# A hybrid attention and HGRN2 layer on one core: the query projection moved behind the last HGRN head, twelve opening matmuls on a constant tile, first loads reordered

## The chip, the cores and the metric

The kernel runs on one core of one Trainium2 chip. The metric is the device time of one execution in microseconds, as the median of several runs. The engines are named as the profile names them: PE is TensorE (matrix products, PEld its weight loads), DVE is VectorE, ACT is ScalarE, POOL is GpSimd, SP is SyncE, whose queue issues all the DMAs here.

## The reference, cut to what matters

One decoder layer over 1024 tokens of width 1024. The input projection makes the queries `q` (512 columns), three pairs of keys and values of 128 columns each for the compressed (`kc_raw`, `vc_raw`), selected and window branches, 24 gate logits, and four blocks of 512 columns for the HGRN2 heads.

```python
h = rms_norm(x, norm_mix[l])
proj = h @ w_in[l]
(q, kc_raw, vc_raw, ks, vs, kw, vw, gate_logits, hq, hf, hi, hg) = jnp.split(proj, split_points, axis=-1)
q = rms_norm(q.reshape(B, T, H, dh), q_norm[l])
kc = rms_norm(compress(kc_raw..., cmp_pos_k[l], cmp_k_w1[l], cmp_k_w2[l]), k_norm[l, 0])
vc = compress(vc_raw..., cmp_pos_v[l], cmp_v_w1[l], cmp_v_w2[l])
...
o_nsa = nsa_mixer(q, kc, vc, ks, vs..., kw, vw..., gates)
o_hgrn = hgrn2_mixer(hq, hf, hi, hg, lower_bounds[l], hgrn_o_norm[l])
x = x + jnp.concatenate([o_nsa, o_hgrn], axis=-1) @ w_out[l]
h = rms_norm(x, norm_ffn[l])
gate, up = jnp.split(h @ w_gate_up[l], 2, axis=-1)
x = x + (jax.nn.silu(gate) * up) @ w_down[l]
```

The queries are needed first by the attention blocks, the norms of the queries too; HGRN2 does not use them.

## The kernel before, in words

Every product in float32 accuracy is made of three products of split operands: `split` (lines 107 to 114) makes a rounded high part on ACT and the rest on DVE, and `mm3` (lines 116 to 119) issues high x high, high x low and low x high into one PSUM bank. So the lines 117, 118 and 119 are those of nearly all matmuls, 110 and 111 those of weight splits (113 and 114 of the transposed input).

The program runs in this order.

1. **Opening and wide stages** (pool `p0`). `step(c)` loads chunk c of the transposed input (`x_in`) into a page of `kv1` and splits it into `hT_h` and `hT_l`. `wide(n0, ...)` takes 512 columns of `w_in` for all eight token tiles at once, one PSUM bank each, chunk by chunk: 8 chunks x 8 tiles x 3 = 192 matmuls. It is called for the gate columns of HGRN (`C_HG`, line 319), the queries (`C_Q`, line 320) and the values of HGRN (`C_HI`, line 321). `ev_q` (line 311) evacuates a query tile into `qtok` on ACT, squares it on POOL (line 314) and sums it by heads on DVE (line 315); the last tile is followed by `rsqrt` into `rs_q`.
2. **HGRN heads 0 to 3** (pool `hg`, lines 438 to 465). `dim_tile` makes a head's columns, `hgrn_head` runs seven levels (`lv`): each has four 128x128 products on PE (line 381), whose operands ACT has gathered (line 377), and on DVE and POOL two scalings (lines 386, 387), one product of `fp` (line 389) and two masked copies into the head's matrix `At` (line 392). Eight transposes (line 399), state products (line 406), output products (lines 418, 420), a norm, and eight closing transposes (line 435) with their evacuation (line 436) follow. `At` is page 4 or 5 of `kv1`, by the head's parity; page 7 is `rs_b`, the broadcast row scale, last read by the head's first steps.
3. **Compressed branch** (pool `cp`, from line 511 on, opened after `hg` is closed). `tok_group` makes 256 columns for the compressed branch (`C_KC`: keys and values; eight token tiles of 24 matmuls, one after the other through the two banks `a0` and `a1` that `acc()` gives in turn), `ev_c` (line 516) evacuates them into two tiles `kcv` of pool `cp`. `comp_gather(which)` transposes them, copies them into `kk` (lines 535, 543, 545) and multiplies by `w1t` (line 557); `comp_gelu` and `comp_out` follow. Between these stand the groups for window and selected keys and values (`kv_group`), their norms (`keys_norm`) and transposes (`keys_out`).
4. **Attention blocks**, out projection, norm and feed-forward part.

A scheduler sets each engine's order: it may move an instruction ahead of others where its operands allow it, and keeps the written order otherwise as a priority. A tile waits until the memory it takes over is free: `cp` takes over what `hg` leaves. Weight pages come from a ring of eight (`wring`), raw loads from three pages (`raw`).

## Time and profile before

| | us |
|---|---|
| median of three runs | 1428.98 |
| lowest and highest run | 1428.91, 1430.2 |
| the profiled execution's own time | 1426.9 |
| its span, first to last instruction | 1424.9 |
| TensorE busy | 1374.1 |
| VectorE busy | 1048.4 |
| ScalarE busy | 597.3 |
| GpSimd busy | 390.6 |

The span is that of one profiled execution; its own time has 2.0 us more around it. Busy times add up durations on one engine, so what bounds the kernel at a place is read from that place: from the stretches, the waits and the timeline there.

### The profile page before, as it was taken

The numbers are of one execution on the slowest core, as the hardware profiler recorded it, in microseconds if no ns is written. First come the engines' busy times: TensorE is split into PE (matmuls) and PEld (weight loads), VectorE is DVE, ScalarE is ACT, GpSimd is POOL, SyncE is SP. The second block draws the span as 40 slices with busy tenths as digits, with TensorE's granted clock in tenths as the row PEclk, the third lists the DMA queues.
The fourth block names the chain that finished last, engine by engine and source line by source line (L and its number), as shares of the span: only waits on it lengthen the run. The fifth ranks groups of instructions, "written<-read, shape, count | busy, mean of one in ns | idle before, by whom it ended". The sixth has DMA issues, their size and how long they took to land.

```text
span 1424.9 us, 19708 instructions
## 1 busy us (share of the span) xinstructions
PE 1374.1 (96%) x7080; PEld 1135.3 (80%) x7080; DVE 1048.4 (74%) x1895; ACT 597.3 (42%) x1156; POOL 390.6 (27%) x341
## 2 busy tenths in 40 slices
PE   8999999969999999999998999999999999999998
PEld 6888788859987778777776788888888888887787
DVE  5331588872777887888876898888888887589864
ACT  7222233313436666666664433333333333443342
POOL 0020011110025442434354533233323320058500
PEclk9999999979999999999999999999999999999999
DMA  9311110102130001100003233333333337997431
GB/s 339 106 45 46 44 28 21 30 1 75 47 134 1 1 1 32 43 31 16 30 16 89 67 112 111 111 111 101 99 112 97 111 111 245 328 323 277 150 109 59
DMA packets 108625, 135.72 MB, mean 95 GB/s; under 512 B 6096, under 2 KB 63600, under 8 KB 108528
## 3 DMA queue, kind: packets, MB, share of 16 engines
q1 hardware_dynamic: 108528, 134.46, 28.3%
q8 instruction: 56, 0.92, 0.3%
q14 instruction: 41, 0.34, 0.1%
HBM read 105.87 MB, written 28.57 MB: 94 GB/s over the span
## 4 chain that ended last, share of the span: by engine, by line
PE 83%; DVE 11%; ACT 3%; issue 2%; POOL 1%; DMA 1%; SPq 0%; ACTq 0%; POOLq 0%; DVEq 0%
PE bank L117 9%; PE bank L118 9%; PE bank L119 9%; PE a L117 8%; PE a L118 8%; PE a L119 8%; PE ps_t L118 4%; PE ps_t L119 4%; PE ps_t L117 4%; PE ps_t L846 3%; PE a L850 2%; DVE wop L111 2%; PE a L851 2%; PE ps_t L381 2%; PE ps_s L824 1%
## 5 line engine op out<-in xcount | busy, mean ns | idle before, releaser
L110 ACT ACTIVATE wop<-rpage 128x512 fp32r<-128x512 f32 x140 | 87.6, 629 | 190.9 <-PE a L119 78.6
L835 POOL TENSOR_SCALAR pbig<-pbig,den,gates 128x640 f32<-128x640 f32 (+7 forms) x128 | 104.0, 817 | 165.7 <-DVE den L834 146.5
L111 DVE TENSOR_TENSOR wop<-rpage,wop 128x512 fp32r<-128x512 f32 x140 | 106.9, 766 | 49.7 <-ACT wop L110 47.7
L849 DVE TENSOR_TENSOR ph<-ps_t,ph 128x512 fp32r<-128x512 f32 x126 | 84.3, 683 | 17.8 <-ACT ph L848 17.0
L848 ACT ACTIVATE ph<-ps_t 128x512 fp32r<-128x512 f32 x126 | 72.7, 596 | 48.9 <-PE ps_t L846 39.2
L846 PE MATMUL ps_t<-ident,pbig 128*128 128x128 f32 x504 | 78.2, 274 | 2.1 <-POOL pbig L835 2.1
L111 DVE TENSOR_TENSOR wop<-act_a,wop 128x512 fp32r<-128x512 f32 x48 | 47.4, 988 | 32.5 <-ACT wop L110 32.5
L387 POOL TENSOR_TENSOR kp<-kp,fp 128x256 f32<-128x256 f32 x28 | 20.0, 716 | 183.9 <-PE bank L364 129.7
L997 POOL TENSOR_TENSOR tmp<-tmp,rpage 128x512 f32<-128x512 f32 x21 | 31.2, 1488 | 142.4 <-DVE wop L111 142.4
L846 PEld LDWEIGHTS ps_t<-ident,pbig 128*128 128x128 f32 x504 | 60.6, 140 | 11.6 <-POOL pbig L835 3.2
L111 DVE TENSOR_TENSOR wlo<-wraw,whi 128x1024 fp32r<-128x1024 f32 (+2 forms) x23 | 27.1, 1182 | 54.2 <-ACT whi L110 22.5
L833 ACT ACTIVATE pbig<-ps_s,nm 128x640 f32<-128x640 f32 (+3 forms) x64 | 55.9, 875 | 23.5 <-DVE nm L832 17.8
L118 PE MATMUL bank<-wop 128*128 128x512 f32 x165 | 64.9, 394 | 0.0
L117 PE MATMUL bank<-wop 128*128 128x512 f32 x165 | 64.9, 393 | 0.0
L119 PE MATMUL bank<-wop 128*128 128x512 f32 x165 | 64.7, 392 | 0.0
L110 ACT ACTIVATE wop<-act_a 128x512 fp32r<-128x512 f32 x48 | 30.3, 631 | 81.4 <-PE bank L119 56.6
L832 DVE TENSOR_REDUCE nm<-ps_s 128x1 f32<-128x640 f32 (+3 forms) x64 | 58.1, 913 | 4.4 <-PE ps_s L827 3.0
L850 PE MATMUL a<-ph,kv 128*128 128x512 f32 x132 | 58.6, 444 | 2.0 <-ACT ph L848 1.2
L851 PE MATMUL a<-ph,kv 128*128 128x512 f32 x132 | 56.9, 431 | 3.2 <-DVE ph L849 2.7
L111 DVE TENSOR_TENSOR wop<-tmp,wop 128x512 fp32r<-128x512 f32 x42 | 43.6, 1039 | 20.6 <-ACT wop L110 20.0
L957 POOL TENSOR_TENSOR tmp<-rpage 128x512 f32<-128x512 f32 x20 | 26.0, 1301 | 112.9 <-DMA rpage<-in_w_gate_up_dram 112.9
L110 ACT ACTIVATE wop<-tmp 128x512 fp32r<-128x512 f32 x42 | 26.6, 634 | 70.4 <-POOL tmp L997 37.5
(457 smaller groups left out, 4458.1 us busy)
## 6 DMA issues: line engine op xcount, KB each, us to landing
rpage<-in_w_gate_up_dram SPq DMA_DIRECT2D x86, 256.0 KB, 3.1
raws<-in_w_down_dram SPq DMA_DIRECT2D x35, 512.0 KB, 7.2
act_a<-act_d SPq DMA_DIRECT2D x12, 1024.0 KB, 6.2
act_d<-as SPq DMA_DIRECT2D x33, 256.0 KB, 2.1
act_e<-act_d SPq DMA_DIRECT2D x6, 1024.0 KB, 8.0
act_d<-tmp SPq DMA_DIRECT2D x22, 256.0 KB, 2.1
act_d<-th SPq DMA_DIRECT2D x22, 256.0 KB, 2.1
xn<-in_x_dram SPq DMA_DIRECT2D x8, 512.0 KB, 5.3
```

What stands on the lines that cost most here:

```text
L110: A.activation(hi, src, AF.Copy)
L111: V.tensor_tensor(lo, src, hi.bitcast(F32), op=OP.subtract)
L117: PE.matmul(o, ah, bh, start=first, stop=False, skip_group_check=chained)
L118: PE.matmul(o, ah, bl, start=False, stop=False, skip_group_check=chained)
L119: PE.matmul(o, al, bh, start=False, stop=last, skip_group_check=chained)
L832: V.tensor_reduce(nm, sv, axis=AX.XY, op=OP.max, negate=True)
L835: G.tensor_scalar(pp, pp, den, gates[:, qb, h * 3 + 1 + b:h * 3 + 2 + b], op0=OP.mult, op1=OP.mult)
L846: PE.transpose(pt[:, r * P:(r + 1) * P], wts[r][:, c0:c0 + P], ident)
L848: A.activation(ph[:, 0], pt, AF.Copy)
L849: V.tensor_tensor(ph[:, 1], pt, ph[:, 0].bitcast(F32), op=OP.subtract)
L850: PE.matmul(o, vst[b][:, kb, g, :], ph[:, 0], start=b == 0 and kb == kb0, stop=False)
L851: PE.matmul(o, vst[b][:, kb, g, :], ph[:, 1], start=False, stop=False)
```

## The change

It does four things. The wide query stage and the squares in it are taken out of the opening; the queries are made by `tok_group` instead, tiles 0 to 3 behind the compressed columns, tiles 4 and 5 after the first gelu, 6 and 7 after the second, and their squares follow in `query_norms`. The compressed columns' group moves into the HGRN pool's block, and `kcv` becomes pages 4 and 7 of `kv1`. The window key groups come after the queries, and `comp_keys` is called earlier. At the opening a constant tile is filled and twelve matmuls are made on it into PSUM banks whose content nothing reads; the first weight tile is loaded ahead of the first chunk of x, and that chunk is loaded in pieces of 256, 256 and 512 columns. One line more at the top moves all line numbers, which are in the new file one higher up to the opening.

```diff
@@ -38,6 +38,7 @@
 EXTRA = 1
 LATE = 4
 KEEP = 0
+WARM = 12
 NFIRST = 2
 EARLY = (-4, -3, -2, -1)
 C_Q, C_KC, C_VC, C_KS, C_VS, C_KW, C_VW, C_G, C_HQ, C_HF, C_HI, C_HG = (
@@ -250,6 +251,11 @@
         ssx = p0.tile([P, NT], F32, name="ssx")
         nc.sync.dma_start(par_t, par)
 
+        warm = p0.tile([P, 512], BF16, name="warm")
+        V.memset(warm, 1.0)
+        for _ in range(WARM):
+            PE.matmul(ps_t(), warm[:, 0:P], warm, start=True, stop=True)
+
         def x_stats(t):
             xn = p0.tile([P, D], F32, name="xn", tag="xn", bufs=2)
             nc.sync.dma_start(xn, x[0, t * P:(t + 1) * P, :])
@@ -258,11 +264,10 @@
                 rsqrt(rsx, ssx, NT, 1.0 / D, EPS)
                 V.tensor_scalar(rsh, rsx, 0.5, None, op0=OP.mult)
 
-        def x_in(c, pieces):
-
-            w = T // pieces
-            for k in range(pieces):
-                sl = slice(w * k, w * (k + 1))
+        def x_in(c, cuts):
+
+            for k0, k1 in zip(cuts, cuts[1:]):
+                sl = slice(k0, k1)
                 nc.sync.dma_start(kv1[:, 4 + c % 4, sl], x_t[c * P:(c + 1) * P, sl])
                 split(hT_h[:, c, sl], hT_l[:, c, sl], kv1[:, 4 + c % 4, sl], gmx[:, c:c + 1])
 
@@ -280,9 +285,9 @@
             banks = [bank8() for _ in range(NT)]
             ws = w_steps(n0, fine)
             for c in range(NK):
+                wh, wl = next(ws)
                 if step:
                     step(c)
-                wh, wl = next(ws)
                 for t in range(NT):
                     mm3(banks[t], hT_h[:, c, t * P:(t + 1) * P], hT_l[:, c, t * P:(t + 1) * P], wh, wl,
                         c == 0, c == NK - 1)
@@ -290,7 +295,7 @@
                         evac(t, banks[t])
 
         def step(c):
-            x_in(c, 2 if c == 0 else 1)
+            x_in(c, (0, 256, 512, T) if c == 0 else (0, T))
             if c >= 2:
                 x_stats(c - 2)
 
@@ -306,18 +311,7 @@
             V.scalar_tensor_tensor(gmix[:, :, t * P:(t + 1) * P], th.rearrange("p (h n) -> p h n", h=4), 1.0,
                                    a.rearrange("p (h n) -> p h n", h=4), op0=OP.add, op1=OP.mult)
 
-        ssq = p0.tile([P, 64], F32, name="ssq")
-
-        def ev_q(t, a):
-            A.activation(qtok[:, t, :], a, AF.Copy, scale=rsx[:, t:t + 1])
-            jq = p0.tile([P, 512], F32, name="jq", tag="th", bufs=2)
-            G.tensor_tensor(jq, qtok[:, t, :], qtok[:, t, :], op=OP.mult)
-            V.tensor_reduce(ssq[:, t * 8:(t + 1) * 8], jq.rearrange("p (h d) -> p h d", d=DH), axis=AX.X, op=OP.add)
-            if t == NT - 1:
-                rsqrt(rs_q, ssq, 64, 1.0 / DH, EPS)
-
         wide(C_HG, ev_g, step, True)
-        wide(C_Q, ev_q)
         wide(C_HI, ev_v)
 
         for k in range(2):
@@ -435,6 +429,14 @@
                 PE.transpose(st[:, c * P:(c + 1) * P], qp[:, (4 * k + c) * P:(4 * k + c + 1) * P], ident)
             A.activation(gmix[:, h, sl], st, AF.Copy, scale=og)
 
+    def queries(order, group, parts=None):
+
+        def ev(t, a):
+            A.activation(qtok[:, t, :], a, AF.Copy, scale=rsx[:, t:t + 1])
+        parts = parts or in_units([(C_Q, 512)], 512, (0, 2, 4, 6, 8))
+        group(parts, 512, ev, order, acc)
+        return parts
+
     with tc.tile_pool(name="hg", bufs=2) as hp:
         def head(h):
             fp = hp.tile([P, T], F32, name="fp")
@@ -464,6 +466,13 @@
         head(2)
         head(3)
 
+        def ev_c(t, a):
+            A.activation(kcv[t // 4].rearrange("p (t n) -> p t n", n=256)[:, t % 4], a[:, 0:256], AF.Copy,
+                         scale=rsx[:, t:t + 1])
+        kcv = kv1[:, 4, :], kv1[:, 7, :]
+        tok_group(in_units([(C_KC, 256)], 256), 256, ev_c)
+        parts_q = queries(range(4), tok_group)
+
 
     dram = ctx.enter_context(tc.tile_pool(name="dram", bufs=1, space=bass.MemoryType.DRAM))
     x1_d = dram.tile([T, D], F32, name="x1_d")
@@ -510,11 +519,6 @@
 
     with tc.tile_pool(name="cp", bufs=1) as cp:
         kcn = cp.tile([P, GROUPS, P], F32R, name="kcn")
-        kcv = [cp.tile([P, 4, 256], F32, name=f"kcv{k}") for k in range(2)]
-
-        def ev_c(t, a):
-            A.activation(kcv[t // 4][:, t % 4], a[:, 0:256], AF.Copy, scale=rsx[:, t:t + 1])
-        tok_group(in_units([(C_KC, 256)], 256), 256, ev_c)
         V.memset(kcn.bitcast(F32), 0.0)
         V.memset(kc_st.bitcast(F32), 0.0)
         V.memset(vc_st.bitcast(F32), 0.0)
@@ -546,7 +550,7 @@
             for hf in range(2):
                 pt = ps_t()
                 for t in range(4):
-                    src = kcv[hf][:, t, which * P:(which + 1) * P]
+                    src = kcv[hf][:, 256 * t + which * P:256 * t + (which + 1) * P]
                     if t % 2:
                         PE.matmul(pt[:, t * P:(t + 1) * P], src, swap, start=True, stop=True)
                     else:
@@ -601,9 +605,13 @@
             V.tensor_copy(kc_st[:, 0:128].rearrange("p (g n) -> p g n", g=GROUPS),
                           pk[:, 0:256].rearrange("p (g n) -> p g n", g=GROUPS)[:, :, 0:64])
 
-        kv2 = big.tile([P, NK, T], F32R, name="kv2", tag="KV")
-        kst = {(b, g): kv2[:, 2 * b + g, :] for b in range(2) for g in range(GROUPS)}
-        vst = [kv2[:, 4 + 2 * b:6 + 2 * b, :].rearrange("p a (t g e) -> p (a t) g e", t=4, g=GROUPS) for b in range(2)]
+        def query_norms():
+            ssq = small.tile([P, 64], F32, name="ssq", tag="ssq", bufs=1)
+            for t in range(NT):
+                jq = cp.tile([P, 512], F32, name="jq", tag="jq", bufs=2)
+                G.tensor_tensor(jq, qtok[:, t, :], qtok[:, t, :], op=OP.mult)
+                V.tensor_reduce(ssq[:, t * 8:(t + 1) * 8], jq.rearrange("p (h d) -> p h d", d=DH), axis=AX.X, op=OP.add)
+            rsqrt(rs_q, ssq, 64, 1.0 / DH, EPS)
 
         def kv_weights(b):
             ncols = (256, 280)[b]
@@ -651,19 +659,26 @@
 
         ph0, w20 = comp_gather(0)
         w0 = comp_gelu(ph0)
-        parts1 = kv_weights(1)
-        kraw10 = kv_group(1, 0, parts1)
+        queries((4, 5), tok_group, parts_q)
         ph1, w21 = comp_gather(1)
         comp_out(0, w0, w20)
         w1 = comp_gelu(ph1)
+        queries((6, 7), tok_group4, parts_q)
+        comp_out(1, w1, w21)
+        kv2 = big.tile([P, NK, T], F32R, name="kv2", tag="KV")
+        kst = {(b, g): kv2[:, 2 * b + g, :] for b in range(2) for g in range(GROUPS)}
+        vst = [kv2[:, 4 + 2 * b:6 + 2 * b, :].rearrange("p a (t g e) -> p (a t) g e", t=4, g=GROUPS) for b in range(2)]
+
+        query_norms()
+        parts1 = kv_weights(1)
+        kraw10 = kv_group(1, 0, parts1)
+        comp_keys()
+        kd10 = keys_norm(1, 0, kraw10)
         kraw11 = kv_group(1, 1, parts1)
-        comp_out(1, w1, w21)
-        kd10 = keys_norm(1, 0, kraw10)
+        keys_out(1, 0, kd10)
         parts0 = kv_weights(0)
         kd11 = keys_norm(1, 1, kraw11)
         kraw00 = kv_group(0, 0, parts0)
-        keys_out(1, 0, kd10)
-        comp_keys()
         keys_out(1, 1, kd11)
         kd00 = keys_norm(0, 0, kraw00)
         kraw01 = kv_group(0, 1, parts0)
```

Three places of the engines' orders, first as they were and then as they are.

TensorE in HGRN head 3, from the first level on (line 381, in the new file 375, is a level's products; `a_2356` and `a_2095` are banks of the compressed columns, lines 117 to 119 and 118 to 120 their three products). Before:

```order
L381 MATMUL ps_t<-qp,kv_86 128x128 x4
L117 MATMUL a_2356<-whi,hT_h 128x256
L118 MATMUL a_2356<-wlo,hT_h 128x256
L119 MATMUL a_2356<-whi,hT_l 128x256
L117 MATMUL a_2356<-whi,hT_h 128x256
L118 MATMUL a_2356<-wlo,hT_h 128x256
L119 MATMUL a_2356<-whi,hT_l 128x256
L381 MATMUL ps_t<-qp,kv_86 128x128 x24
L399 MATMUL bank<-ident,kp 128x128 x8
L406 MATMUL bank<-kv_86,kp 128x128 x7
L418 MATMUL bank<-kv_86 128x128 x2
```

After:

```order
L375 MATMUL ps_t<-qp,kv_86 128x128 x4
L120 MATMUL a_2095<-whi,hT_l 128x256
L118 MATMUL a_2095<-whi,hT_h 128x256
L119 MATMUL a_2095<-wlo,hT_h 128x256
L120 MATMUL a_2095<-whi,hT_l 128x256
L118 MATMUL a_2095<-whi,hT_h 128x256
L119 MATMUL a_2095<-wlo,hT_h 128x256
L120 MATMUL a_2095<-whi,hT_l 128x256
L118 MATMUL a_2095<-whi,hT_h 128x256
L375 MATMUL ps_t<-qp,kv_86 128x128 x4
L119 MATMUL a_2095<-wlo,hT_h 128x256
L120 MATMUL a_2095<-whi,hT_l 128x256
```

The other six levels stood back to back; now matmuls of the compressed columns stand between each two of them, and in the same way ahead of the closing transposes.

TensorE around head 3's closing transposes (line 435, now 429; `a_2382` is the third tile of the compressed columns, `a_2225` the seventh). Before:

```order
L420 MATMUL bank<-fp,qp 128x128
L435 MATMUL bank<-ident,qp 128x128 x8
L117 MATMUL bank<-whi,hT_h 128x280
L118 MATMUL bank<-wlo,hT_h 128x280
L119 MATMUL bank<-whi,hT_l 128x280
L117 MATMUL bank<-whi,hT_h 128x280
L118 MATMUL bank<-wlo,hT_h 128x280
L117 MATMUL a_2382<-whi,hT_h 128x256
L118 MATMUL a_2382<-wlo,hT_h 128x256
```

After:

```order
L120 MATMUL a_2225<-whi,hT_l 128x256
L118 MATMUL a_2225<-whi,hT_h 128x256
L119 MATMUL a_2225<-wlo,hT_h 128x256
L429 MATMUL bank<-ident,qp 128x128 x4
L120 MATMUL a_2225<-whi,hT_l 128x256
L429 MATMUL bank<-ident,qp 128x128 x4
L118 MATMUL a_2225<-whi,hT_h 128x256
L119 MATMUL a_2225<-wlo,hT_h 128x256
```

The third compressed tile stood behind the transposes, and the first key matmuls ahead of it; now the first six tiles and a part of the seventh stand ahead of them.

VectorE at the first gathering of `kk` (lines 535 and 545, now 539 and 549; line 613 sums the squares of a query tile, lines 501 and 502 split the first part of the mixed output). Before:

```order
L501 CAST rpage<-gmix 128x512
L535 COPY kk<-ps_t 128x16
L502 TENSOR_TENSOR rpage<-gmix,rpage 128x512
L111 TENSOR_TENSOR wlo<-wraw,whi 128x1024
L545 COPY kk<-ps_t 64x8x31
L545 COPY kk<-ps_t 64x8x32
```

After:

```order
L613 TENSOR_REDUCE ssq<-jq 128x8 x3
L539 COPY kk<-ps_t 128x16
L549 COPY kk<-ps_t 64x8x31
L613 TENSOR_REDUCE ssq<-jq 128x8
L549 COPY kk<-ps_t 64x8x31
L549 COPY kk<-ps_t 64x8x32
```

The sums of the query squares of tiles 0 to 2 now stand ahead of these copies, that of tile 3 between the first copy and the others.

## Rows read from the trace of the kernel before

**Rows 1.** the page: span; busy time, share of the span and instructions of each engine.

```profile
span 1424.9 us, 19708 instructions
PE 1374.1 (96%) x7080; PEld 1135.3 (80%) x7080; DVE 1048.4 (74%) x1895; ACT 597.3 (42%) x1156; POOL 390.6 (27%) x341
```

**Rows 2.** stretches: length, busy PE, PEld, DVE, ACT, POOL, granted clock, DMA share, GB/s.

```profile
300.00:310.00 10.00, 8.37 (x43) 7.74 (x44) 5.95 (x21) 1.91 (x4) 1.25 (x2) 0.58 0.01 2
310.00:320.00 10.00, 3.38 (x30) 3.20 (x29) 7.25 (x23) 1.20 (x2) 0.00 (x0) 0.76 0.00 0
```

**Rows 3.** who TensorE waited for, 280 to 345 us: total, times, longest.

```profile
PE bank L435 <- DVE qp L432: 6.8, 2, 6.6
PE ps_t L381 <- DVE qp L386: 2.6, 3, 1.4
PE ps_t L381 <- ACT kv L377: 2.0, 1, 2.0
PE ps_t L381 <- DVE fp L389: 1.9, 2, 0.9
```

**Rows 4.** timeline of ScalarE, 318 to 330 us: start, duration, operation.

```profile
322.23 0.83 ACT L516 ACTIVATE kcv<-a,rsx 128x256 f32<-128x256 f32 x2
```

**Rows 5.** timeline of TensorE, head 3 and the groups behind it.

```profile
297.60 2.04 PE L381 MATMUL ps_t<-qp,kv 128*128 128x128 f32 x8 [0.94 <-DVE qp L386]
...
305.41 1.92 PE L399 MATMUL bank<-ident,kp 128*128 128x128 f32 x8
...
323.12 0.41 PE L118 MATMUL a<-wlo,hT_h 128*128 128x256 f32 x1
...
325.45 0.28 PE L117 MATMUL a<-whi,hT_h 128*128 128x256 f32 x1
...
334.08 0.28 PE L117 MATMUL a<-whi,hT_h 128*128 128x256 f32 x1
```

**Rows 6.** timeline of TensorE in head 2, the same operations.

```profile
261.09 1.07 PE L381 MATMUL ps_t<-qp,kv 128*128 128x128 f32 x8
...
264.52 1.04 PE L399 MATMUL bank<-ident,kp 128*128 128x128 f32 x8
```

**Rows 7.** who TensorE waited for, 160 to 280 us (heads 0 to 2).

```profile
PE ps_t L381 <- DVE qp L386: 1.8, 3, 0.6
```

**Rows 8.** timeline of TensorE at the opening.

```profile
6.75 0.79 PE L117 MATMUL a<-wop,hT_h 128*128 128x512 f32 x1 [6.75 <-ACT wop L110]
...
12.20 0.39 PE L119 MATMUL bank<-wop,hT_l 128*128 128x512 f32 x1
...
14.47 0.39 PE L117 MATMUL a<-wop,hT_h 128*128 128x512 f32 x1
```

**Rows 9.** timeline of ScalarE at the opening.

```profile
3.94 1.33 ACT L113 ACTIVATE hT_h<-kv,par_t 128x512 fp32r<-128x512 f32 x2 [0.64 <-DMA kv<-in_x_t_dram]
6.07 0.63 ACT L110 ACTIVATE wop<-rpage 128x512 fp32r<-128x512 f32 x1 [0.80 <-DMA rpage<-in_w_in_dram]
8.56 1.15 ACT L113 ACTIVATE hT_h<-kv,par_t 128x1024 fp32r<-128x1024 f32 x1 [1.85 <-DMA kv<-in_x_t_dram]
```

**Rows 10.** timelines of POOL and VectorE in head 2.

```profile
254.00 0.73 POOL L387 TENSOR_TENSOR kp<-kp,fp 128x256 f32<-128x256 f32 x1 [2.40 <-DVE fp L389]
...
252.34 0.42 DVE L387 TENSOR_TENSOR kp<-kp,fp 128x256 f32<-128x256 f32 x1
...
254.22 0.79 DVE L387 TENSOR_TENSOR kp<-kp,fp 128x256 f32<-128x256 f32 x1
```

**Rows 11.** timeline of POOL, 88 to 112 us: the squares of the queries.

```profile
92.28 8.04 POOL L314 TENSOR_TENSOR jq<-qtok 128x512 f32<-128x512 f32 x8 [90.63 <-ACT qtok L312]
```

**Rows 12.** timelines of VectorE and TensorE in the compressed branch.

```profile
342.47 1.22 DVE L111 TENSOR_TENSOR wlo<-wraw,whi 128x1024 fp32r<-128x1024 f32 x1
343.60 2.47 DVE L545 COPY kk<-ps_t 64x248 f32<-64x248 f32 x6
...
347.26 0.93 PE L557 MATMUL ps_t<-kk,w1t 128*128 128x127 f32 x6 [0.30 <-DVE kv L622]
```

## The prediction

> **What bounds the kernel now.** I read the page first. TensorE is busy 1374.1 us, 96% of the span of 1424.9 [rows 1], so some 51 us are to be had at most by closing its gaps; no other engine comes near. The question for a change that only moves matmuls is then where those gaps lie, and whether the moved matmuls land in one. The stretches of ten microseconds answer it: the opening has nothing on TensorE for 6.75 us [rows 8], heads 0 to 2 are nearly full, and from 290 to 320 us, behind the last HGRN head's start, TensorE is busy 8.37 us of ten in one stretch and 3.38 in the next, at a mean granted clock of 0.58 and 0.76 [rows 2]. Those means are of 1.2 and 2.4 GHz: one clock for part of the stretch, the other for the rest.
>
> The list of waits says who holds TensorE there: between 280 and 345 us it stands 6.8 + 2.6 + 2.0 + 1.9 = 13.3 us, all of it for VectorE and ScalarE work of head 3 itself, with one wait of 6.6 us in front of the head's closing transposes (line 435) [rows 3]. So head 3 is a chain of seven levels that hops between engines, and TensorE has nothing else to do meanwhile. Why not, when the token groups of the compressed columns (KC below, eight tiles of 24 matmuls) are independent of it? The reader should look at ScalarE: the first two KC tiles stand in TensorE's order ahead of head 3's last levels, yet their evacuation to `kcv` runs only at 322.23 us [rows 4], behind the head's closing transposes. `kcv` lives in pool `cp`, opened where `hg` closes, so it stands in the memory of head 3's own tiles. Two PSUM banks `a0` and `a1` stay full, and tiles 2 to 7 cannot start.
>
> **The part that fills the gap.** The change puts `kcv` into pages 4 and 7 of `kv1` (free once head 2's `At` and the last read of `rs_b` are done) and writes the queries' groups for tiles 0 to 3 behind KC. The order printed above shows the outcome: between head 3's levels there are now 8, 15, 11, 9, 8 and 8 KC matmuls, 52 between its last products and the closing transposes, and query groups behind. The work itself costs the same as where it was: 192 matmuls of 512 columns, at the step of (14.47 - 12.20) / 10 = 0.227 us [rows 8], are 43.6 us that leave the wide stage and come back later. So the gain is the gap and not the work:
> - idle time removed: 13.3 us [rows 3];
> - matmuls that ran at 1.2 GHz because of it and will run at 2.4: four level groups at 2.04 instead of 1.07, 3.9 us; eight transposes at 1.92 instead of 1.04, 0.9 us; and eleven KC matmuls, 323.12 to 325.45, at 0.212 instead of the later (334.08 - 325.45) / 72 = 0.120, 1.0 us [rows 5, 6]. The shorter cold groups around them (the state products, the closing transposes, five key matmuls) hold about 1.5 more, an estimate by the same factor. Together 7.3;
> - idle time that stays: a level leaves a wait of 0.94 [rows 5] and gets at least 8 x 0.120 = 0.96 us of KC; the 6.6 us wait gets 52 x 0.120 = 6.2. Heads 0 to 2, filled in just this way, still wait 1.8 us for level products, 0.6 a head [rows 7]. The first levels, with waits up to 2.0 [rows 3] against 1.3 to 1.8 of fill, add some. I take 2.0 in all; the ends are 0.6 and, if twice the estimate, 4.
>
> That is 13.3 + 7.3 - 2.0 = 18.6 us gained.
>
> **What is late next.** With the queries behind the head, the squares and sums for their norms (POOL and VectorE) leave an idle stretch and enter the compressed branch. VectorE's row for tile 3's sum now stands between the first copy into `kk` and the seven others. That sum needs ScalarE's evacuation, 1.33 / 2 = 0.67 for 512 columns [rows 9], then POOL's square, 8.04 / 8 = 1.0 us [rows 11], then the sum itself, which I take as long as the evacuation. So the copies go on some 2.6 us (with the hand-overs) after the tile's last matmul and, at 2.47 / 6 = 0.41 us each [rows 12], end near 5.5 us. TensorE covers this with eight transposes, 1.04 us by [rows 6] and rather 1.5 as half of them are products with `swap`, and 17 query matmuls, 3.9 us: 5.4. The first product that reads `kk` already waits 0.30 us today [rows 12]. It happens twice, for keys and values: I add 0.6 us in all, between 0 and 3. A VectorE op next to a POOL op is also slower: the same form takes 0.79 us with POOL beside it and 0.42 alone [rows 10], so eight squares cost VectorE at most about 8 x 0.37 = 3 us, which only matters if it falls on those copies; that is where my 3 comes from. The Trainium skill (SBUF — State Buffer, section Who interferes with whom) says more sharply that a VectorE instruction with two SBUF inputs and a GpSimd one that reads SBUF exclude each other for the whole instruction; the copies come from PSUM and would be spared, but a square could be held behind a weight split (1.22 us [rows 12]), and by that rule the sum would be worse by up to 2 x 1.22 = 2.4 us. No row here shows POOL held so; I stay with the rows.
>
> The four query weight loads (512 KB each) stand on SP's queue ahead of `w1t`, which waits for head 3's end; the third and fourth need ring pages that KC's last tile frees. Their split ends some 2.4 us after KC (an estimate), while c = 4 of the first query tile is reached after 12 x 0.227 = 2.7 us: hidden, at worst 1 us. `w1t` itself is needed only after 21.8 us of queries. Removing the wide query stage from the front costs nothing: TensorE has work without a break on both sides of it, and the value columns simply follow the gate columns into the same eight banks. Matmuls from head 0 to head 2 are in the order they had, and so are those from the first attention block on.
>
> **The opening.** Now the first matmul starts at 6.75 us and the 24 matmuls of chunk 0 last until 14.47, 7.72 us instead of 24 x 0.227 = 5.45 [rows 8]. The excess of 2.27 is ten matmuls at the lower clock: the clock rose some 4.5 us after the first. The twelve matmuls on a constant need only a fill that VectorE does first, near 1 us. Ten at 0.45 and two at 0.23 make 5.0 us, so they end near 6.1. The weight tile, issued first instead of behind the first x pieces, lands before today's 6.07, and the first quarter of x soon after today's 3.94 [rows 9], so chunk 0 is ready by then. It would end at 6.1 + 5.45 = 11.6: 2.9 us gained. Chunk 1's x comes at 8.56 today [rows 9] and has one 256 KB weight tile more ahead of it, about half of 6.07 - 3.94, so 9.6; ScalarE's 1.15 and VectorE's like time bring it to 12, where its third matmul needs it. A slip there takes 0.5. Ends: if the twelve do not bring the clock up early, 0; if they run one by one, with 0.7 us from start to start, the first real matmul slips to 9.6 and 0.6 us is lost; at best 3.2.
>
> **Sum.** 18.6 + 2.9 - 0.6 = 20.9 us. The profiled execution took 1426.9 us, of which 1424.9 are span; that becomes 1406.0. The median of the runs, 1428.98, stands 2.1 us above the profiled one, and I predict for the median: **1408 us**. The likeliest case's own range is 1405 to 1412.
>
> **Rivals.**
> - *The opening yields nothing* (chance 0.09): 1411, or 1411.6 with the loss. For: the rows tell that the clock rose after 4.5 us of real matmuls, not that ones on a constant count the same. Against: to TensorE nothing else differs.
> - *The fill is too thin and the clock still falls in head 3* (0.08). Idle doubles (2 us), four level groups and the transposes stay cold (4.8), and some 60 KC matmuls between them run at 0.212 (5.5): 12 us back, 1420. For: the fill is exact to a tenth of a microsecond. Against: heads 0 to 2 with equal waits.
> - *The change does not free the banks* (0.03): some other dependence of `kcv` on `kv1` holds the evacuations as now. Only the opening is left: 1426.7. Against: the new ScalarE order has KC evacuations between the levels.
> - *Slower* (0.03): query groups run one at a time through banks `a0` and `a1`, each emptied by ScalarE before its next turn. If TensorE pauses at each turn and the clock falls through all 192 query matmuls, they cost 192 x 0.227 = 44 us more: 1452. It decides from 24 us of that on, 105 matmuls at 1.2 GHz. Against: KC tiles use just these two banks at 0.120 us a step for 72 steps on end [rows 5]. The Trainium skill (TensorE: Matmul & The Clock Gate, section A second HAM failure mode: psum-queue depth-cycling) reports a kernel whose cycling through banks made the clock swing; by that rule this rival would win, and the trace so far speaks against it.
>
> **Numbers.** Likeliest 0.77, rivals 0.09, 0.08, 0.03, 0.03. A difference of 0.2% (2.9 us) is about what a measurement of this kernel tells from none. Faster: the first three, 0.94; same: 0.03, the third rival at the border; slower 0.03. The range runs from 1404 to 1415: it takes in the ends of idle, copies and opening and the lost opening, and leaves out most of the thin fill and the last two.
>
> **What would show it.** In the changed profile the wait in front of the closing transposes should fall from 6.6 to under 1 us; KC evacuations should stand between head 3's levels; the granted clock should be 1.00 through head 3 and the queries, and the 512-column step 0.23 us from the first real matmul on, with chunk 0 ending near 11.6 us. The first product on `kk` should wait under 1 us, twice. I am wrong if TensorE's idle time from head 3's start to the window keys exceeds about 6 us, or if the clock falls there.

## The result

The changed kernel takes 1405.2 us (median of four runs, 1403.4 to 1406.5) against 1429.6 for the kernel before (four runs, 1428.9 to 1430.5): a ratio of 0.9828, with a 95% interval of 0.9811 to 0.9845. The forecast of 1408 was 2.8 us too high; the time lies in its range. The profiled executions differ by 1426.9 - 1406.5 = 20.4 us, their spans by 20.3. Of the 14 later runs of the kernel before, one took 4110.3 us; it is left out wherever they are compared.

### The profile page after: what moved, and what is told of

Read it like the earlier page. It is cut to its first block, busy times and chain, and to the rows that moved or that the text cites. A ratio compares the mean times of both kernels' runs of the same rounds, so it can differ in the third digit from the quotient of the medians.

```text
span 1404.6 us, 19716 instructions
## 1 busy us (share of the span) xinstructions
PE 1371.6 (98%) x7092; PEld 1129.5 (80%) x7092; DVE 1048.0 (75%) x1893; ACT 596.5 (42%) x1153; POOL 392.1 (28%) x341
## 4 chain that ended last, share of the span: by engine, by line
PE 82%; DVE 12%; ACT 2%; issue 2%; POOL 1%; DMA 1%; SPq 0%; ACTq 0%; POOLq 0%; DVEq 0%
PE bank L118 9%; PE bank L119 9%; PE bank L120 9%; PE a L118 8%; PE a L120 8%; PE a L119 8%; PE ps_t L119 4%; PE ps_t L120 4%; PE ps_t L118 4%; PE ps_t L861 3%; PE a L865 2%; DVE wop L112 2%; PE a L866 2%; PE ps_t L375 1%; PE ps_s L839 1%
## 5 line engine op out<-in xcount | busy, mean ns | idle before, releaser
L111 ACT ACTIVATE wop<-rpage 128x512 fp32r<-128x512 f32 x132 | 82.7, 630 | 156.9 <-PE bank L120 70.7
L112 DVE TENSOR_TENSOR wop<-rpage,wop 128x512 fp32r<-128x512 f32 x132 | 100.7, 765 | 14.6 <-ACT wop L111 12.7
L864 DVE TENSOR_TENSOR ph<-ps_t,ph 128x512 fp32r<-128x512 f32 x126 | 84.3, 683 | 18.5 <-ACT ph L863 17.6
L381 POOL TENSOR_TENSOR kp<-kp,fp 128x256 f32<-128x256 f32 x28 | 20.3, 725 | 232.8 <-PE bank L358 181.3
L112 DVE TENSOR_TENSOR wlo<-wraw,whi 128x1024 fp32r<-128x1024 f32 (+2 forms) x27 | 32.0, 1188 | 46.0 <-PE a L120 19.3
```

The source lines that it names most:

```text
L111: A.activation(hi, src, AF.Copy)
L112: V.tensor_tensor(lo, src, hi.bitcast(F32), op=OP.subtract)
L864: V.tensor_tensor(ph[:, 1], pt, ph[:, 0].bitcast(F32), op=OP.subtract)
```

## The profile after

The page of the changed kernel, span and busy time, against [rows 1]:

```profile
span 1404.6 us, 19716 instructions
...
PE 1371.6 (98%) x7092; PEld 1129.5 (80%) x7092; DVE 1048.0 (75%) x1893; ACT 596.5 (42%) x1153; POOL 392.1 (28%) x341
```

TensorE has twelve instructions more, the matmuls on the constant, and is busy 2.5 us less: the span shrank by idle time and by matmuls that no longer ran at the lower clock. The stretches of head 3, which stands at 234.0 to 269.5 us now, against [rows 2]:

```profile
237.00:247.00 10.00, 9.79 (x82) 9.37 (x81) 9.01 (x17) 3.01 (x8) 2.71 (x3) 1.00 0.27 89
247.00:257.00 10.00, 9.49 (x76) 8.73 (x75) 9.44 (x31) 4.22 (x12) 2.57 (x4) 1.00 0.01 3
257.00:267.00 10.00, 10.00 (x89) 10.00 (x88) 6.47 (x23) 1.92 (x4) 0.00 (x0) 1.00 0.00 0
267.00:277.00 10.00, 9.62 (x71) 8.93 (x70) 4.51 (x6) 4.73 (x7) 0.00 (x0) 1.00 0.44 121
```

The first pair of numbers behind the length is TensorE's, the 1.00 near the end the granted clock. Where 8.37 and 3.38 us were busy at mean clocks of 0.58 and 0.76, every stretch is above 9.4 at 1.00. The list of TensorE's waits from 230 to 345 us, against [rows 3]:

```profile
PE ps_t L375 <- DVE qp L380: 0.4, 1, 0.4
PE ps_t L561 <- ACT kk L547: 0.4, 2, 0.2
PE bank L429 <- DVE qp L426: 0.4, 1, 0.4
PE ps_t L375 <- ACT kv L371: 0.2, 1, 0.2
```

Head 3 itself waits 0.4 + 0.4 + 0.2 us where it waited 13.3, and the closing transposes (line 429, before line 435) 0.4 where they waited 6.6. The second row is the first product on `kk`, twice. ScalarE's timeline shows what let go, against [rows 4]; these are the first five evacuations of KC:

```profile
239.19 0.46 ACT L470 ACTIVATE kv<-a,rsx 128x256 f32<-128x256 f32 x1
...
243.95 0.46 ACT L470 ACTIVATE kv<-a,rsx 128x256 f32<-128x256 f32 x1
...
249.46 0.46 ACT L470 ACTIVATE kv<-a,rsx 128x256 f32<-128x256 f32 x1
...
256.78 0.48 ACT L470 ACTIVATE kv<-a,rsx 128x256 f32<-128x256 f32 x1
...
264.42 0.47 ACT L470 ACTIVATE kv<-a,rsx 128x256 f32<-128x256 f32 x1 [2.09 <-PE a L120]
```

They stand among head 3's levels (240.1 to 254.9 us) and ahead of its closing transposes (268.24); before, the first two waited for the head's end. TensorE's timeline of the levels, against [rows 5]:

```profile
245.27 1.16 PE L375 MATMUL ps_t<-qp,kv 128*128 128x128 f32 x8 [0.21 <-ACT kv L371]
...
247.82 1.13 PE L375 MATMUL ps_t<-qp,kv 128*128 128x128 f32 x8 [0.45 <-DVE qp L380]
...
268.24 0.66 PE L429 MATMUL bank<-ident,qp 128*128 128x128 f32 x4 [0.39 <-DVE qp L426]
```

A level group takes 1.13 to 1.16 us where the slow ones took 2.04, and these three are the only ones in the head with an idle time ahead of them. The opening, against [rows 8]:

```profile
1.45 4.59 PE L257 MATMUL ps_t<-warm 128*128 128x512 bf16 x12 [1.45 <-DVE warm L255]
5.69 0.58 PE L118 MATMUL a<-wop,hT_h 128*128 128x512 f32 x1
6.11 0.40 PE L118 MATMUL ps_t<-wop,hT_h 128*128 128x512 f32 x1
6.34 0.39 PE L119 MATMUL a<-wop,hT_h 128*128 128x512 f32 x1
...
11.90 0.39 PE L118 MATMUL a<-wop,hT_h 128*128 128x512 f32 x1
```

The matmuls on the constant begin at 1.45, and from 6.11 on the steps are 0.23 us. The second chunk starts at 11.90 instead of 14.47. Between 8.4 and 10.1 us a few steps are longer than 0.23: x's third piece is late, as ScalarE's timeline shows (against [rows 9]):

```profile
7.96 0.72 ACT L114 ACTIVATE hT_h<-kv,par_t 128x512 fp32r<-128x512 f32 x1 [2.08 <-DMA kv<-in_x_t_dram]
```

The opening differs from one profile to the next: in three kernels with the old opening its second chunk starts at 14.47, 15.31 and 13.82 us. So the experiments are read by marks in the trace as well as by times. Four starts on TensorE and the span, in us: the eighth chunk of the opening, the first product of head 3, the first matmul of the first attention block, the end. The eighth chunk's first matmul is the 169th of the wide stage; the expectations below give this mark too early by two to four matmuls, 0.45 to 0.91 us: their 46.2, 47.3 and 45.6 are 47.1, 48.0 and 46.5 here, their 44.0, 43.4 and 44.0 are 44.9, 44.0 and 44.9. "Middle" is the attention block's start less the eighth chunk's, "rest" is the end less the attention block's start.

| kernel | eighth chunk | head 3 | attention | end | middle | rest |
|---|---|---|---|---|---|---|
| before | 47.11 | 280.97 | 417.63 | 1424.9 | 370.5 | 1007.3 |
| changed | 44.93 | 234.00 | 394.65 | 1404.6 | 349.7 | 1010.0 |
| kcv alone freed | 47.95 | 281.85 | 399.99 | 1405.7 | 352.0 | 1005.7 |
| kcv alone put back | 44.04 | 233.12 | 412.88 | 1418.7 | 368.8 | 1005.8 |
| queries back in the wide stage | 44.88 | 278.39 | 397.44 | 1403.3 | 352.6 | 1005.9 |
| queries alone moved | 46.46 | 235.67 | 396.67 | 1403.8 | 350.2 | 1007.2 |
| opening alone | 44.08 | 277.63 | 415.02 | 1422.5 | 370.9 | 1007.5 |
| no constants | 45.86 | 234.98 | 395.65 | 1403.1 | 349.8 | 1007.4 |
| old loads | 44.93 | 234.07 | 395.07 | 1403.6 | 350.1 | 1008.5 |
| queries and opening | 44.04 | 233.21 | 393.87 | 1401.0 | 349.8 | 1007.1 |

The change gains 23.0 us by the attention block's start (417.63 to 394.65) and gives 2.7 back behind it, where every engine has the same work in the same order.

## The experiments

The theory was that of the prediction: `kcv`'s memory kept ScalarE from emptying two banks, so nothing could fill head 3. The rival was that the queries, moved behind the head, are what fills it or what is needed besides. Four kernels separate the two, four runs each (one of them profiled) beside seven runs of the kernel before (median 1428.9).

**kcv alone freed.** The kernel before, with one line moved from pool `cp` to the pool of the whole program:

```
+    kcv = [gpool.tile([P, 4, 256], F32, name=f"kcv{k}") for k in range(2)]
...
-        kcv = [cp.tile([P, 4, 256], F32, name=f"kcv{k}") for k in range(2)]
```

> The kernel before, with one edit: the two kcv tiles get memory of their own, so that they no longer lie in the pool that opens behind the last head. Queries and opening stay as before. Theory 1 (what kept head 3 unfilled was that the evacuations of KC could not start before its pool's memory came free, so the banks did not come free either): KC's eight 256-column groups run between head 3's levels, TensorE's wait before the closing transposes falls from 6.6 us to under 1, the granted clock stays at 1.00 there, and the attention block starts 12 to 20 us before its 417.5 (20 if nothing behind the head takes KC's place as a wait; 12 if the load of the compressed weights, about 6 us behind the head, is now bare). Time 1409 to 1417. Rival (the 512-column queries are what fills): the wait stays at 5 us or more and the time is within 3 us of before.

Measured: 1408.6 us (1406.2 to 1409.8), ratio 0.9859 [0.9844, 0.9874]: a gain of 20.2 us for one moved allocation, with queries and opening as before. Its waits on TensorE, 278 to 350 us:

```profile
PE ps_t L534 <- DMA post<-in_cmp_pos_k_dram: 1.1, 1, 1.1
PE bank L436 <- DVE qp L433: 0.6, 2, 0.4
PE ps_t L557 <- ACT kk L543: 0.5, 1, 0.5
```

The closing transposes (line 436 here) wait 0.4 at most. The first row is what now stands bare behind the head: a small load for the compressed branch lands 1.1 us late, which in the kernel before was hidden by KC. The attention block starts 17.6 us early, and the time is 0.4 below the lower end of what was expected. The theory holds, the rival falls: the queries are not needed for the gap.

**kcv alone put back.** The changed kernel with the two tiles, KC's groups and the first four query groups in the later pool again:

```
-        kcv = kv1[:, 4, :], kv1[:, 7, :]
-        tok_group(in_units([(C_KC, 256)], 256), 256, ev_c)
-        parts_q = queries(range(4), tok_group)
...
+        kcv = [cp.tile([P, 1024], F32, name=f"kcv{k}") for k in range(2)]
...
+        tok_group(in_units([(C_KC, 256)], 256), 256, ev_c)
+        parts_q = queries(range(4), tok_group)
```

> The changed kernel, with one part undone: kcv goes back into the pool that opens behind the last head, and KC and the first four query groups are called there. Opening, the queries' place behind the head and all else stay changed. Theory 1 (kcv's memory decides): head 3 is bare again, TensorE waits about 6.6 us before the closing transposes, the clock falls in the 20 us of the head, and the attention block starts only 2 to 5 us before 417.5; time 1422 to 1427. Rival (queries anywhere near the head are enough): attention starts about 20 us early, time 1404 to 1410.

Measured: 1422.0 us (1420.5 to 1423.4), ratio 0.9955 [0.9940, 0.9969]; the attention block starts 4.8 us early. Its waits from 230 to 340 us, and ScalarE's timeline behind the head:

```profile
PE bank L429 <- DVE qp L426: 6.6, 1, 6.6
PE ps_t L375 <- DVE qp L380: 2.3, 2, 1.4
PE ps_t L375 <- DVE fp L383: 1.9, 2, 0.9
PE ps_t L375 <- ACT kv L371: 1.7, 1, 1.7
PE a L118 <- ACT kcv L519: 1.1, 1, 1.1
```

```profile
271.72 0.69 ACT L430 ACTIVATE gmix<-bank,gains 128x512 f32<-128x512 f32 x1 [0.17 <-PE bank L429]
272.30 0.83 ACT L519 ACTIVATE kcv<-a,rsx 128x256 f32<-128x256 f32 x2
```

That is the gap of [rows 3] again, 12.5 us of waits in the first four rows, 6.6 of them ahead of the same transposes, and KC's first evacuation right behind the head's last one, as in [rows 4]. The last row is the full bank itself: TensorE's next KC matmul waits for that evacuation. The queries can't help here, since they are written behind KC and take the same two banks after it. From the eighth chunk to the attention block this kernel needs 368.8 us and the changed one 349.7. So the gap costs 19.1 us by this pair, and 370.5 - 352.0 = 18.5 by the pair without the queries' move.

**Queries back in the wide stage.** The changed kernel without the move of the queries:

```
+        wide(C_Q, ev_q)
...
-        parts_q = queries(range(4), tok_group)
...
-        queries((4, 5), tok_group, parts_q)
...
-        queries((6, 7), tok_group4, parts_q)
...
-        query_norms()
```

> The changed kernel, with the queries back in the opening's wide stage; kcv's memory and the opening stay changed. Theory 1 (KC fills head 3, the queries only stand behind it): head 3 stays closed (wait before the closing transposes under 1 us, clock 1.00), and the time differs from the changed kernel only by what the queries cover behind the head: 0 to 7 us more, 1404 to 1412. Rival (the queries are the filler of head 3): the gap returns, 1422 to 1427.

Measured: 1406.3 us (1405.4 to 1407.6), ratio 0.9848 [0.9832, 0.9865], which overlaps the changed kernel's interval of 0.9811 to 0.9845. Head 3 is as full as there. By the marks the queries' place is worth 397.44 - 44.88 less 394.65 - 44.93, 2.8 us, and the waits from 275 to 350 us show where:

```profile
PE ps_t L571 <- ACT kk L557: 1.4, 2, 0.9
PE ps_t L548 <- DMA post<-in_cmp_pos_k_dram: 1.1, 1, 1.1
```

Behind the head, 1.4 and 1.1 us stand bare here that the query groups hide in the changed kernel (0.4 and none). The theory holds.

**Queries alone moved.** The kernel before with the query groups behind head 3 and their norms behind the first gelu; `kcv` stays in the later pool:

```
-        wide(C_Q, ev_q)
...
         head(3)
+        queries(range(NT), tok_group)
...
+        query_norms()
```

> The kernel before, with the queries alone moved: all eight 512-column query groups are called behind head 3, kcv stays in the later pool, the opening stays as before, the query norms come behind the first gelu. Theory 1 (any column work whose banks come free can fill): the queries run between head 3's levels, wait before the closing transposes under 1 us, clock 1.00, attention starts 17 to 20 us before 417.5, time 1408 to 1412. Rival (only KC's thin groups fit between the levels, or 512 columns in two alternating banks let the clock fall): attention starts less than 10 us early, or later; time over 1419.

Measured: 1406.4 us (1405.2 to 1408.7), ratio 0.9848 [0.9833, 0.9862]: 22.4 us gained with the old opening, 1.6 us beyond the best end of what was expected. The waits from 232 to 340 us are the shortest list of all, and ScalarE's timeline shows the queries' evacuations in the levels' midst:

```profile
PE ps_t L370 <- DVE qp L375: 0.5, 1, 0.5
PE bank L424 <- DVE qp L421: 0.3, 1, 0.3
```

```profile
242.85 0.69 ACT L430 ACTIVATE qtok<-a,rsx 128x512 f32<-128x512 f32 x1 [0.88 <-PE a L119]
...
254.58 0.69 ACT L430 ACTIVATE qtok<-a,rsx 128x512 f32<-128x512 f32 x1
```

`qtok` has lain in memory of its own all along, so these banks come free. Both kinds of column work that were tried, KC and the queries, fill head 3 once their destination is writable by then. That 512-column groups fit is shown too, and that two alternating banks don't bring the clock down here: its stretches from 232 to 292 us all show 1.00. This speaks against the prediction's rival on cycling banks a second time. The section that the prediction cited (the Trainium skill, TensorE: Matmul & The Clock Gate, section A second HAM failure mode: psum-queue depth-cycling) tells of a TensorE that idles between the groups; here, behind the head, the groups follow one another without a wait and the evacuations run beside them, so the cycling alone didn't cost the clock and the section's case did not arise.

For the opening and for the parts together, four kernels beside 13 runs of the kernel before (median 1428.7).

**Opening alone.** The kernel before with the constants, the load order and the three pieces of x:

```
+WARM = 12
...
+        for _ in range(WARM):
+            PE.matmul(ps_t(), warm[:, 0:P], warm, start=True, stop=True)
...
+                wh, wl = next(ws)
                 if step:
                     step(c)
-                wh, wl = next(ws)
...
-            x_in(c, 2 if c == 0 else 1)
+            x_in(c, (0, 256, 512, T) if c == 0 else (0, T))
```

> The kernel before with the opening's edits alone: twelve matmuls on a constant tile, the weight piece asked for ahead of the x pieces, x in three pieces. Landmark: TensorE's first matmul of the eighth chunk, which stood at 46.2, 47.3 and 45.6 us in three kernels with the old opening (mean 46.3) and at 44.0, 43.4 and 44.0 in three with the new (mean 43.8). Theory (the opening is worth about 2.6 us, and nothing later takes it back): eighth chunk at 43.3 to 44.3, time 1425.5 to 1427.0. Rival (head 3 or the loads behind it take it back, since they don't depend on the opening): eighth chunk as in the theory, but the attention block's start within 1 us of 417.6 and the time within 1 us of before.

Measured: 1424.2 us (eight runs, 1422.3 to 1425.2), ratio 0.9970 [0.9960, 0.9980]. The eighth chunk starts at 44.08, 3.0 us before that of the kernel before, and the attention block at 415.02, 2.6 us before it; the middle takes 370.9 us against 370.5: nearly nothing takes the opening back, the rival falls. The median is 4.5 us below, 1.9 more than the marks and 1.3 below the lower end of what was expected. In the profiled runs the difference is 1426.9 - 1424.5 = 2.4; the rest of the median's gain stands in executions without a trace and stays open.

**No constants**, and **old loads**: the changed kernel with one half of the opening undone.

```
-WARM = 12
+WARM = 0
```

> The changed kernel without the matmuls on the constant tile; the new order and pieces of the loads stay. Theory (the constants carry most of the opening's gain, since the first real matmuls then run at the higher clock): the first real matmul stays near 5.7 us, the steps are 0.42 us instead of 0.23 for the first 4 us or so, and the eighth chunk starts at 45.3 to 46.0; time 1.5 to 2.2 us above the changed kernel. Rival (the loads carry it): eighth chunk within 0.5 us of 43.8 and the time that of the changed kernel.

```
-                wh, wl = next(ws)
                 if step:
                     step(c)
+                wh, wl = next(ws)
...
-            x_in(c, (0, 256, 512, T) if c == 0 else (0, T))
+            x_in(c, (0, 512, T) if c == 0 else (0, T))
```

> The changed kernel with the old order of loads (x's two pieces of 512 columns ahead of the weight piece); the matmuls on the constant tile stay. Theory (the constants carry most): the first real matmul is near 6.8 us as in the kernel before, the steps 0.23 us from the start, and the eighth chunk starts at 44.3 to 45.0; time 0.5 to 1.2 us above the changed kernel. Rival (the loads carry it): eighth chunk at 45.5 or later. A third way: a pause between the constants' end (6.0 us) and the first real matmul lets the clock fall again, steps of 0.42 us, eighth chunk at 46 or later.

Measured: 1405.0 us (1404.7 to 1405.7) without the constants and 1405.5 (1403.6 to 1409.5) with the old loads. Neither time can be told from the changed kernel's; the times decide nothing here, the marks do. The first matmuls without constants, and then with the old loads:

```profile
5.11 0.79 PE L118 MATMUL a<-wop,hT_h 128*128 128x512 f32 x1 [5.11 <-ACT hT_h L114]
5.70 0.63 PE L119 MATMUL a<-wop,hT_h 128*128 128x512 f32 x1
...
10.40 0.45 PE L118 MATMUL bank<-wop,hT_h 128*128 128x512 f32 x1
10.69 0.39 PE L119 MATMUL bank<-wop,hT_h 128*128 128x512 f32 x1
```

```profile
6.71 0.50 PE L118 MATMUL a<-wop,hT_h 128*128 128x512 f32 x1 [0.29 <-ACT wop L111]
...
8.67 0.39 PE L119 MATMUL ps_t<-wop,hT_h 128*128 128x512 f32 x1
8.89 0.39 PE L120 MATMUL ps_t<-wop,hT_l 128*128 128x512 f32 x1
```

Without constants the steps are 0.43 us until 10.4, and the eighth chunk starts at 45.86, 1.2 behind the mean of the three kernels first read with the new opening (44.6): short of the theory's 1.5 to 2.2, but 0.9 behind the latest of the five that have the whole new opening (44.04 to 44.93). The loop of constants has its own price: real work could start at 5.11 and starts at 5.69, since twelve matmuls take longer than the loads. With the old loads the first real matmul is at 6.71, as before, but soon after it the steps are 0.23 us, those of the high clock; the eighth chunk starts at 44.93, 0.3 behind the mean and as late as the changed kernel's. So of the 2.6 us from the old opening (mean 47.2) to the new one, the constants alone bring 47.2 - 44.9 = 2.2, the loads alone 47.2 - 45.9 = 1.3, and together they overlap. These are single profiles, and the three with the old opening spread over 1.5 us (46.46 to 47.95): that the constants carry most is shown by the steps and the marks, the loads' own share is not clear of the spread. The pause of 0.3 us between the constants and the first matmul does not cost the clock.

**Queries and opening**, without freeing `kcv`: the edits of two experiments above, together.

> The kernel before with the queries alone moved, and the new opening: kcv stays in the later pool, all eight query groups stand right behind head 3. If the gains add, as the theory has it: the eighth chunk at 43.3 to 44.3, from there to the attention block's start 351 us (351.1 with the queries alone moved, 350.6 in the changed kernel), so a start at 394.3 to 395.3 and a time of 1403 to 1405, the changed kernel's within 1.5 us: then freeing kcv's memory is worth nothing beside queries that stand right behind the head. Rival (the changed kernel needs both): 2 us or more above the changed kernel.

Measured: 1403.2 us (1402.4 to 1404.9), ratio 0.9828 [0.9815, 0.9841], the changed kernel's ratio to four places; eighth chunk at 44.04, attention block at 393.87, middle 349.8 against 349.7. The gains add, and freeing `kcv` is worth nothing beside queries that stand right behind the head. No version measured beats the changed kernel by more than the runs spread.

## Why the prediction was right

Its steps in order, measured to the attention block's start.

- **What holds the gap.** Right: `kcv`'s memory, with the banks behind it. Freed alone it gains 18.5 us of the middle, put back alone it costs 19.1.
- **The gap, idle and cold: 13.3 + 7.3.** Right in kind, and 2.4 us too low with the two terms below. From head 3's start to the attention block the kernel before took 417.63 - 280.97 = 136.7 us and the changed one 160.7 with 43.5 us of queries in it (eight tiles at 5.44 us, the step of ScalarE's evacuations at 280.03, 285.47 and 290.91). The kernel before had made ten matmuls of KC by head 3's start, the changed one three; the seven, at 0.12 us, are 0.8. So the same work took 136.7 and 116.3: 20.4 gained, where 18.6 - 0.6 = 18.0 was forecast. TensorE's waits in this stretch add up to 15.0 and 2.9 us, 12.1 fewer where 13.3 - 2.0 - 0.6 = 10.7 was forecast. The other 8.3 is what the lower clock had cost, by difference, where the forecast had 7.3.
- **The idle time that stays, 2.0.** Too high: 0.21 + 0.45 + 0.39 = 1.05 us in the profile after. Heads 0 to 2 had waited 2.5 us and not 1.8, since [rows 7] leaves out 0.7 before their closing transposes.
- **The copies into `kk`, 0.6 lost.** Wrong in sign, small: the two waits are 0.4 in all, against 0.30 [rows 12] and a second one of 0.2 before: 0.1 gained. The order had the sum of squares ahead of seven copies, and the trace shows it there:

```profile
297.80 0.41 DVE L549 COPY kk<-ps_t 64x248 f32<-64x248 f32 x1 [1.10 <-ACT kk L547]
298.19 0.69 DVE L613 TENSOR_REDUCE ssq<-jq 128x8 f32<-128x512 f32 x1
298.91 2.66 DVE L549 COPY kk<-ps_t 64x248 f32<-64x248 f32 x6
```

 It costs 0.7 us on VectorE, and the query matmuls cover all but 0.19.
- **POOL's squares held by VectorE.** The prediction had this as possible, with no row for it; one of the eight squares was held. Seven take 1.04 to 1.07 us, the eighth 2.44. POOL's row, then VectorE's two beside it, a cast and a weight split:

```profile
331.65 2.44 POOL L612 TENSOR_TENSOR jq<-qtok 128x512 f32<-128x512 f32 x1 [2.37 <-ACT qtok L435]
```

```profile
331.44 0.41 DVE L510 CAST rpage<-gmix 128x512 fp32r<-128x512 f32 x1
...
331.98 1.20 DVE L112 TENSOR_TENSOR wlo<-wraw,whi 128x1024 fp32r<-128x1024 f32 x1
```

 Its own 1.04, the 0.20 that the cast still ran and the split's 1.20 make just 2.44, as if POOL stood still while they lasted: 1.4 us of the 2.4 that the prediction had worked out. With kcv alone put back, without constants and with the old loads it is 2.60, 2.43 and 2.60 beside the same two. For the split this agrees with the Trainium skill's rule as the prediction gave it (SBUF — State Buffer, section Who interferes with whom). It goes the other way too: a VectorE product of two operands in SBUF, 128 columns wide, took 1.02 us beside the seventh square, which had begun before it, and 0.28 in the kernel before. The held square cost TensorE nothing: from 325 to 395 us it waits once, 1.4 us for a key tile, as the kernel before does.
- **The queries leave the wide stage at no cost.** Right: in both kernels the chunks of the wide stages start 5.44 us apart, so the queries' eight took 43.5 us there and take as much behind the head. From the eighth chunk to head 3 it is 233.9 us before and 189.1 after, 44.8; of the 1.3 beyond 43.5, 0.8 is the seven KC matmuls, which the changed kernel makes later, and the rest, 0.4, shorter waits in heads 0 to 2.
- **The opening, 2.9.** 2.6 at the second chunk: ScalarE waited 2.08 us for x's third piece, where the forecast had all of chunk 0 ready in time. 2.2 at the third and still at the eighth: the slip of up to 0.5 at chunk 1's third matmul, which the forecast had named, took 0.4. The fill ended at 1.45 us, where near 1 was put without a row, and the twelve matmuls took 4.59 us where 5.0 was worked out; no run shows the 0.7 us from start to start of the bad end.
- **The sum.** 2.2 + 0.4 + 20.4 = 23.0 by the attention block's start, where 20.9 had been forecast; 2.7 went behind it, which leaves 20.3 in the profiled pair. That this lies so near 20.9 is luck: the gap was 2.4 us too low and the opening 0.7 too high, and a loss that no term had took the rest. By the medians the gain is 24.4: the changed kernel's profiled run is the slowest of its four (1406.5 of 1403.4 to 1406.5), that of before was below all its four.
- **The rivals.** The opening that yields nothing, the thin fill, the unfreed banks and the cycling banks all fell by the first profile. The unfreed banks are what the second experiment built: 1422.0, where 1426.7 was worked out. Its attention block starts 4.8 us before that of the kernel before, 3.1 of them from the opening and 1.7 from the middle, where the waits of the gap are 12.5 instead of 13.3 us; the remainder was not traced.

## What to carry to other kernels

When a stretch of TensorE is empty though independent work is written right behind it, look at where that work's result goes: a destination in memory that a running stage still holds can keep the PSUM banks full, and one allocation moved was here worth nearly as much as the rearranged program (18.5 of the 20.8 us of the middle). Before moving a large block of work into a gap, try freeing what already stands next to it; here either alone did nearly all, and both together did no more. Changes of two microseconds are read from marks in the trace, each against its own stage, and not from the time.

## What was not expected of the hardware

The rest behind the attention block's start is the same work in the same order in all ten kernels, and takes 1005.7 to 1010.0 us. A part of the difference is in short falls of the granted clock that come at the same few places of the program, in some profiles and not in others. Near 425 us, 30 us into the first attention block, TensorE waits 1.6 us for POOL in the changed kernel and in the kernel with the queries back in the wide stage alike. The stretches of the changed kernel, then of the other:

```profile
422.00:424.00 2.00, 0.58 (x4) 0.21 (x2) 1.52 (x6) 1.62 (x6) 2.00 (x3) 1.00 0.00 0
424.00:426.00 2.00, 1.79 (x12) 1.59 (x12) 1.59 (x5) 1.94 (x7) 2.00 (x5) 0.76 0.00 0
426.00:428.00 2.00, 2.00 (x8) 1.68 (x8) 2.00 (x6) 0.98 (x5) 0.93 (x2) 0.50 0.01 4
```

```profile
424.00:426.00 2.00, 1.01 (x9) 0.69 (x7) 1.59 (x6) 1.70 (x6) 2.00 (x2) 1.00 0.02 4
426.00:428.00 2.00, 1.36 (x10) 1.12 (x10) 1.58 (x7) 1.77 (x8) 2.00 (x5) 1.00 0.00 0
```

The same pause is followed by a fall to half in one and by nothing in the other. In the changed profile stretches of 5 us at a mean of 0.66, 0.66, 0.73 and 0.59 (from 425, 560, 1300 and 1305 us) lose up to 1.7 + 1.7 + 1.35 + 2.05 = 6.8 us; before, behind the attention block's start, 0.83, 0.83 and 0.66 (from 445, 450 and 1325) lose 3.4. The 3.4 between them is about the 2.7 that were given back. So the 2.7 us are put down to the clock and not to the change's work; a single profiled pair of this kernel can be off by as much. The falls are not all of it: with the queries alone moved they come to 5.15 us by the same sum, and the rest takes 1007.2. Why a given pause costs the clock once and not the next time was not tried.

In the first microseconds the granted clock of the view can't be used: without constants it reads 1.00 from 5 to 9 us, where the steps are 0.43 us against 0.23 later.

```profile
5.00:9.00 4.00, 3.89 (x9) 3.15 (x10) 2.66 (x6) 1.94 (x5) 0.00 (x0) 1.00 0.96 353
```

There the step alone tells which clock TensorE has.
